# Latent heads: the rotated query's two halves stacked in one 128-row tile, and gate/value weights used in runs of sixteen products

## The chip, the cores and the metric

The kernel runs on one core of one Trainium2 chip. A core has five engines that each work through their own queue in order: TensorE (PE) multiplies matrices, with its weight loads shown as a row of their own (PEld); VectorE (DVE) and ScalarE (ACT) work element by element; GpSimd (POOL) does a little at the start; SyncE (SP) issues the transfers from the large memory. They wait for each other through semaphores only. The metric is the device time of one execution in microseconds; the kernel before has a median of 2402.7 us over three executions (2402.11 to 2403.8).

## What is computed

A decoder trunk of two layers over 256 tokens of width 2048, all in float32. Layer 0 is dilated window attention (three groups of eight heads) with a gated ConvFFN. Layer 1 is latent attention (twelve heads) over a shared key/value latent, and again a gated ConvFFN. Both also attend to 256 memory tokens. Cut to what the change touches:

```python
# layer 1: a query has a 128-wide part and a rotated 64-wide part; the rotated key is one for all heads
c      = rmsnorm(x, kv_g_norm) @ kv_w_dkv
c_kv   = rmsnorm(c[..., :512], kv_g_latent)
k_rope = rope(c[..., 512:], positions)                       # 64 wide, shared by the 12 heads
k_nope = (c_kv @ kv_w_uk).reshape(B, S, 12, 128)
q      = (cq @ b_w_uq[i]).reshape(B, S, 12, 128 + 64)
q_rope = rope(q[..., 128:], positions)
s = (einsum('bqhe,bkhe->bhqk', q_nope, k_nope)
     + einsum('bqhe,bke->bhqk', q_rope, k_rope)) * scale     # causal mask, softmax, times v

# both layers: the gated ConvFFN
g  = h @ w_gate
gc = conv_b + sum_j shift(g, j) * conv_w[j]
y  = (silu(gc) * (h @ w_val)) @ w_down
```

## The kernel before

**Numbers in two parts.** Every float32 operand is split into hi, its value rounded to the format that TensorE takes (fp32r), and lo, the rest. A product a·b is computed as hi·hi + hi·lo + lo·hi, three passes that add up in one PSUM bank; lo·lo is left out. Activations sit in tiles `op` of [128, 2, 256]: part, then token. Weights come from memory in chunks of 1 MB into a ring of three `raw` buffers and are split there into pieces of [128, 1024]: ACT writes `hi` (L445), DVE writes `lo` (L446), into a ring of four buffers each (`SPLIT_BUFS`). Piece i+4 can be split only when TensorE is done with piece i (`done_piece`).

**How the work is laid out.** `units()` lists the work; each unit is a weight matrix's column block with its pieces. What hangs on a unit (evacuating its bank, rotation, softmax) is recorded as small functions with a due time on a heap; `tick`, called after a product or a few, fires those that are due by the planner's own clock. So the order on each engine is fixed when the program is built, by planned times, and each engine then keeps to it whatever really takes longer.

**Gate and value.** For each of 44 column blocks per layer `unit_gv` takes four pieces: gate and value for the first eight k-tiles, gate and value for the last eight. A wide product multiplies a hi weight with both parts of an activation (512 columns, two of the three passes in one); a narrow one multiplies a lo weight with the hi part (256 columns). Both layers together have 88 such units, 176 halves. In two of them (`inter`, the first of each layer) the runs are of four, since their activations arrive while they run. `unit_wide`, which makes queries and keys of layer 0, has the same products in runs of sixteen wide and sixteen narrow.

**The latent heads.** For each group of four heads come the units `uk` (keys), `uv` (values), `uqr` (rotated queries, two heads side by side in the 128 rows of a bank: 64 rows each) and `uq` (the other part of the query). `rope` rotates a bank and `hilo` splits the result into an `op` tile ("qr", pair). The shared rotated key ("krT") has its 64 rows twice, in rows 0 to 63 and again in 64 to 127, since the unit `kr` loads the same weight columns twice. `mla_scores` then makes a head's scores by `causal_scores`: for the first 128 queries against 128 keys, and for the second against 256 keys, three products over 128 rows (qn·kn) and three over the head's 64 rows (qr·krT). The scores go through mask and maximum (DVE), exponential and scaling (ACT), transposes (PE, into `pth`), and the product with v (PE).

Of the kernel before, what the change touches and what calls it, by code (L numbers as in the profile page):

```python
# [11 lines left out]
F32 = mybir.dt.float32  # L12
F32R = mybir.dt.float32r
I32 = mybir.dt.int32
AF = mybir.ActivationFunctionType
ALU = mybir.AluOpType
AX = mybir.AxisListType

P = 128
T = 256  # L20
D = 2048
KD = D // P
DH = 128
# [4 lines left out]
NOPE = 128  # L28
# [21 lines left out]
LAT_S = 0.5  # L50
PBUFS = 12


# [141 lines left out]
class Core:  # L195
# [467 lines left out]
    def unit_gv(self, ui, u):  # L663
        a = [self.get("acc"), self.get("acc")]
        ops = u["ops"]
        for half in range(2):
            w = [self.take(ui)]
            if u["inter"]:
                w.append(self.take(ui))
                order = [(gv, range(k0, k0 + 4)) for k0 in (0, 4) for gv in range(2)]  # L670
            else:
                order = [(gv, range(8)) for gv in range(2)]
            for gv, ks in order:
                if gv == len(w):
                    self.done_piece()
                    w.append(self.take(ui))
                hi, lo = w[gv]
                for k in ks:
                    X = self.need(ops[8 * half + k])
                    self.mm(a[gv], hi[:, k * P:(k + 1) * P], X.rearrange("p a b -> p (a b)"), 512, half == 0 and k == 0, False)  # L680
                    self.tick()
                for k in ks:
                    X = self.need(ops[8 * half + k])
                    self.mm(a[gv][:, :T], lo[:, k * P:(k + 1) * P], X[:, 0, :], T, False, half == 1 and k == 7)
                    self.tick()
            self.done_piece(2 if u["inter"] else 1)
        _, l, f = u["name"]
        if f == NF - 1:
            self.put(*[("h", 10 + l, k) for k in range(KD)])
        if ("R", 10 + l) in self.T:  # L690
            self.gate(l, f, a)
        else:
            self.at(self.t, lambda: self.gate(l, f, a), keys=[("R", 10 + l)], urgent=True)
# [243 lines left out]

    def rope(self, o, key, half, cos, sin, then, scale=None, wide=False):
        sw, r = self.get("fs"), self.get("fs")
# [17 lines left out]
        def s2():  # L957
            t = self.op(key)
            e = self.hilo(t, T, r, psum=False)
            self.give("fs", r)  # L960
            if then:
                then(e)

        self.at(e + LAT_S, s1)

    def ev_q(self, name, h, o):
# [10 lines left out]
    def a_scores(self, half, g, h):  # L977
# [4 lines left out]
        pi = self.get("p")  # L982
        nm, e = self.causal_scores([(q, k, slice(0, P))], self.ptiles[pi], g, DH ** -0.5, ms)
        self.put(("q", half, g, h), ("k", half, g, h))
# [9 lines left out]
    def causal_scores(self, prods, p, mask, scale, ms):  # L994
        bank = self.get("wk")
        for tt in range(2):
            n = P * (tt + 1)
            o = bank[:, tt * P:tt * P + n]
            qs = slice(tt * P, (tt + 1) * P)
            steps = [(q[rows, i, qs], k[rows, j, 0:n]) for q, k, rows in prods for i, j in ((0, 0), (0, 1), (1, 0))]  # L1000
            for s, (a, b) in enumerate(steps):
# [256 lines left out]
    def ev_uqr(self, name, h, o):  # L1258
        self.rope(o, ("qr", 2 * name[1] + h), ROPE // 2, self.cosB, self.sinB, None)

# [6 lines left out]
    def mla_scores(self, h):  # L1267
        rows = slice((h % 2) * ROPE, (h % 2 + 1) * ROPE)
        pi = self.get("p")
        p = self.ptiles[pi]  # L1270
        ms, l, rl = self.st(2), self.st(2), self.st(2)
        nm, e = self.causal_scores([(self.T[("qn", h)], self.T[("kn", h)], slice(0, P)),
                                    (self.T[("qr", h // 2)], self.T[("krT",)], rows)], p, 3, (NOPE + ROPE) ** -0.5, ms)
        self.put(("qn", h), ("kn", h))
# [99 lines left out]
```

## Time and profile before

| | |
|---|---|
| median of three executions | 2402.7 us |
| the profiled execution: its own time, and its span | 2397.88 us, 2396.0 us |
| busy: PE, PEld, DVE, ACT | 99%, 86%, 66%, 55% of the span |
| mean granted TensorE clock | 0.996 of full speed |
| chain that ended last, by engine | PE 95%, ACT 2%, DVE 1%, DMA 1% |
| layer 0 attention; its FFN | about 55 to 515 us; 595 to about 1330 us |
| latent attention of layer 1 (units uk, uv, uqr, uq) | about 1450 to 1570 us |
| FFN of layer 1 | 1655 us to the end |

The timeline view has one row for a run of like instructions: start, length, engine, line, output and inputs by name, shape (rows x columns), count; in brackets the idle time before it and who ended it. A row's length includes the last instruction's way through the array, so the time of a run is read from its start to the next row's start. `acc<-op,hi` with 512 columns is a wide product, `acc<-op,lo` with 256 a narrow one, `wk<-op,op` are scores, `wk<-pth,op` is attention times v, `wk<-cst,pt` are transposes. The view by windows gives for a stretch each engine's busy time and the granted clock (PEclk).

### The profile page before, as it was taken

The page shows a single profiled execution, that of the slowest core. Times are in us where ns is not written, and L with a number is a line of the kernel's source. Part 1 is how long each engine was busy: PE and PEld are TensorE (multiplying, and loading weights), DVE is VectorE, ACT ScalarE, POOL GpSimd, SP SyncE. Part 2 cuts the span into 40 slices and gives each one's busy share as a digit, 9 for nine tenths or more (in the row PEclk, how much of TensorE's full clock was granted, in tenths as well). Part 3 has the DMA queues.
Part 4 walks back from the last instruction along what each step waited for, and adds up shares of the span by engine and source line. Part 5 has one row for each costly group of instructions (what it writes and reads, how often), then busy time and mean ns, then how long its engine had stood idle before and what let it go on. Part 6 is the DMA issues. An engine that isn't in the chain of part 4 may idle for free.

```text
span 2396.0 us, 33043 instructions
## 1 busy us (share of the span) xinstructions
PE 2377.3 (99%) x12896; PEld 2060.3 (86%) x12896; DVE 1585.0 (66%) x2439; ACT 1310.3 (55%) x2161; POOL 65.6 (3%) x78
## 2 busy tenths in 40 slices
PE   8999999999999999999999999999999999999998
PEld 8988888888888888888888888888888888888887
DVE  7677776665777567765776665656776567755765
ACT  6765665665655445543555656755554345544554
POOL 7300000000000000000000000000000000000000
PEclk9999999999999999999999999999999999999999
DMA  8454444544554555545555553235555555555553
GB/s 324 172 190 176 182 153 176 183 169 159 193 189 183 191 194 192 192 181 200 184 193 183 187 220 141 109 137 181 190 191 188 193 210 184 192 193 193 187 182 141
DMA packets 64749, 441.98 MB, mean 184 GB/s; under 512 B 7248, under 2 KB 7760, under 8 KB 12496
## 3 DMA queue, kind: packets, MB, share of 16 engines
q1 hardware_dynamic: 64592, 439.87, 50.4%
q8 instruction: 101, 1.65, 0.3%
q14 instruction: 56, 0.46, 0.0%
HBM read 437.75 MB, written 2.10 MB: 184 GB/s over the span
## 4 chain that ended last, share of the span: by engine, by line
PE 95%; ACT 2%; DVE 1%; DMA 1%; issue 0%; ACTq 0%; SPq 0%; DVEq 0%
PE acc L336 91%; PE wk L336 3%; DMA raw<-w 1%; PE wk L344 1%; DVE lo L361 1%; ACT hi L348 0%; ACT pt L348 0%; DVE op L361 0%; ACT fs L348 0%; ACT op L348 0%; DVE op L373 0%; DVE fs L361 0%; DVE pth L361 0%; ACT pth L348 0%; ACT junk L348 0%
## 5 line engine op out<-in xcount | busy, mean ns | idle before, releaser
L361 DVE TENSOR_TENSOR lo<-raw,hi 128x1024 fp32r<-128x1024 f32 (+1 forms) x816 | 1000.2, 1230 | 652.5 <-ACT hi L348 626.9
L348 ACT ACTIVATE hi<-raw 128x1024 fp32r<-128x1024 f32 (+1 forms) x816 | 857.5, 1057 | 764.3 <-PE acc L336 638.6
L336 PE MATMUL acc<-op,hi 128*128 128x512 f32 (+1 forms) x4112 | 998.7, 382 | 2.3 <-DVE op L361 2.3
L336 PEld LDWEIGHTS acc<-op,hi 128*128 128x128 f32 x4112 | 732.6, 189 | 125.0 <-DVE op L361 2.0
L336 PE MATMUL acc<-hi,op 128*128 128x512 f32 x2544 | 801.6, 392 | 0.8 <-DVE op L361 0.8
L336 PE MATMUL acc<-op,lo 128*128 128x256 f32 x3912 | 568.6, 282 | 0.8 <-DVE lo L361 0.8
L336 PEld LDWEIGHTS acc<-op,lo 128*128 128x128 f32 x3912 | 539.0, 191 | 33.5 <-DVE lo L361 1.0
L336 PEld LDWEIGHTS acc<-hi,op 128*128 128x128 f32 x2544 | 479.6, 189 | 100.2 <-DVE op L361 1.6
L336 PE MATMUL acc<-lo,op 128*128 128x512 f32 x1272 | 497.1, 391 | 0.9 <-DVE lo L361 0.9
L336 PEld LDWEIGHTS acc<-lo,op 128*128 128x128 f32 x1272 | 239.9, 189 | 49.0 <-DVE lo L361 1.7
L348 ACT ACTIVATE op<-fs 128x256 fp32r<-128x256 f32 x143 | 59.9, 419 | 119.5 <-DVE fs L361 118.9
L361 DVE TENSOR_TENSOR op<-fs,op 128x256 fp32r<-128x256 f32 x143 | 60.6, 424 | 64.3 <-ACT op L348 63.8
L348 ACT ACTIVATE fs<-scr 64x256 f32<-64x256 f32 x96 | 40.1, 418 | 91.5 <-DVE scr L361 90.6
L373 DVE SCALAR_TENSOR_TENSOR fs<-gpad,sml,fs 128x256 f32<-128x256 f32 x176 | 84.8, 482 | 3.1
L361 DVE TENSOR_TENSOR fs<-acc,fs 128x256 f32<-128x256 f32 x176 | 73.4, 417 | 0.0
L348 ACT ACTIVATE fs<-acc 128x256 f32<-128x256 f32 (+1 forms) x204 | 67.0, 373 | 0.4
L361 DVE TENSOR_TENSOR fs<-fs,fs 128x256 f32<-128x256 f32 x143 | 60.3, 421 | 1.9
L336 PE MATMUL wk<-op,op 128*128 128x128 f32 (+1 forms) x336 | 54.1, 295 | 0.0
L348 ACT ACTIVATE fs<-gpad,sml 128x256 f32<-128x256 f32 x88 | 51.9, 589 | 1.7 <-DVE gpad L361 1.6
L336 PEld LDWEIGHTS wk<-op,op 128*128 128x128 f32 x336 | 47.4, 195 | 6.1 <-issue 0.2
L348 ACT ACTIVATE pt<-pt,stat 128x128 f32<-128x128 f32 (+1 forms) x112 | 48.2, 455 | 0.9 <-DVE stat L366 0.9
L361 DVE TENSOR_TENSOR x<-acc,x 128x512 f32<-128x512 f32 (+1 forms) x66 | 41.2, 666 | 3.5 <-PE acc L336 3.5
(107 smaller groups left out, 879.0 us busy)
## 6 DMA issues: line engine op xcount, KB each, us to landing
raw<-w SPq DMA_DIRECT2D x407, 1024.0 KB, 4.8
raw<-w SPq DMA_DIRECT2D x8, 512.0 KB, 4.6
x<-x SPq DMA_DIRECT2D x4, 512.0 KB, 8.4
out<-x SPq DMA_DIRECT2D x8, 256.0 KB, 2.5
x<-w SPq DMA_DIRECT2D x5, 256.0 KB, 4.9
scr<-gfin SPq DMA_DIRECT2D x4, 256.0 KB, 6.5
cst<-cst SPq DMA_DIRECT2D x1, 640.0 KB, 6.7
raw<-w SPq DMA_DIRECT2D x2, 256.0 KB, 3.1
```

Source lines behind the costliest of these rows:

```text
L336: self.nc.tensor.matmul(out, lhsT, rhs, start=start, stop=stop, skip_group_check=True)
L344: self.nc.tensor.transpose(out, in_, self.ident)
L348: self.nc.scalar.activation(out, in_, func, **kw)
L361: self.nc.vector.tensor_tensor(out, a, b, op)
L373: self.nc.vector.scalar_tensor_tensor(out, a, s1, b, op0, op1)
```

## The change

Three things. `unit_gv` takes both pieces of a half at once and issues the eight wide gate products, the eight wide value products, then the eight narrow gate and the eight narrow value products; pieces are given back after the narrow run of each. For the rotated queries `rope` is called with `stack=True`: instead of one split of 128 rows into hi and lo, head b of the pair (rows 64b to 64b+63) gets its hi part in its own rows of plane b of the tile, and its lo part in the other 64 rows of the same plane; two ACT and two DVE instructions of 64 rows instead of one each of 128. And `causal_scores` takes a list of terms per operand pair: for qr·krT now two products over all 128 rows, plane b of the query tile against hi and against lo of the key, so that hi and lo of the query are multiplied in one pass (lo·lo comes with it). Everything else in the planner stays as it was, but its clock runs differently, and so some orders move.

```diff
+THREE = ((0, 0), (0, 1), (1, 0))
...
         for half in range(2):
-            w = [self.take(ui)]
+            w = [self.take(ui), self.take(ui)]
+            runs = [(gv, range(8)) for gv in range(2)]
             if u["inter"]:
-                w.append(self.take(ui))
-                order = [(gv, range(k0, k0 + 4)) for k0 in (0, 4) for gv in range(2)]
-            else:
-                order = [(gv, range(8)) for gv in range(2)]
-            for gv, ks in order:
-                if gv == len(w):
-                    self.done_piece()
-                    w.append(self.take(ui))
-                hi, lo = w[gv]
+                runs = [(gv, range(k0, k0 + 4)) for k0 in (0, 4) for gv in range(2)]
+            for gv, ks in runs:
                 for k in ks:
                     X = self.need(ops[8 * half + k])
-                    self.mm(a[gv], hi[:, k * P:(k + 1) * P], X.rearrange("p a b -> p (a b)"), 512, half == 0 and k == 0, False)
+                    self.mm(a[gv], w[gv][0][:, k * P:(k + 1) * P], X.rearrange("p a b -> p (a b)"), 512, half == 0 and k == 0, False)
                     self.tick()
-                for k in ks:
+            for gv in range(2):
+                for k in range(8):
                     X = self.need(ops[8 * half + k])
-                    self.mm(a[gv][:, :T], lo[:, k * P:(k + 1) * P], X[:, 0, :], T, False, half == 1 and k == 7)
+                    self.mm(a[gv][:, :T], w[gv][1][:, k * P:(k + 1) * P], X[:, 0, :], T, False, half == 1 and k == 7)
                     self.tick()
-            self.done_piece(2 if u["inter"] else 1)
+                self.done_piece()
...
-            e = self.hilo(t, T, r, psum=False)
+            e = self.stack(t, r) if stack else self.hilo(t, T, r, psum=False)
...
+    def stack(self, t, r):
+
+        rows = [slice(i * ROPE, (i + 1) * ROPE) for i in range(2)]
+        for b in range(2):
+            e = self.act(t[rows[b], b, :], r[rows[b]], AF.Copy, T)
+        for b in range(2):
+            e = self.tt(t[rows[b ^ 1], b, :], r[rows[b]], t[rows[b], b, :].bitcast(F32), ALU.subtract, T, e)
+        self.rdy[id(t)] = e + LAT_S
+        return e
...
-            steps = [(q[rows, i, qs], k[rows, j, 0:n]) for q, k, rows in prods for i, j in ((0, 0), (0, 1), (1, 0))]
+            steps = [(q[:, i, qs], k[:, j, 0:n]) for q, k, terms in prods for i, j in terms]
...
-        self.rope(o, ("qr", 2 * name[1] + h), ROPE // 2, self.cosB, self.sinB, None)
+        self.rope(o, ("qr", 2 * name[1] + h), ROPE // 2, self.cosB, self.sinB, None, stack=True)
...
-        nm, e = self.causal_scores([(self.T[("qn", h)], self.T[("kn", h)], slice(0, P)),
-                                    (self.T[("qr", h // 2)], self.T[("krT",)], rows)], p, 3, (NOPE + ROPE) ** -0.5, ms)
+        nm, e = self.causal_scores([(self.T[("qn", h)], self.T[("kn", h)], THREE),
+                                    (self.T[("qr", h // 2)], self.T[("krT",)], ((h % 2, 0), (h % 2, 1)))], p, 3, (NOPE + ROPE) ** -0.5, ms)
```

What this does to the order of instructions is shown at three places. First, TensorE in the middle of a gate/value half, before and after (`hi` and `lo` with a number are buffers of the split rings, `acc_141` gathers the gate and `acc_142` the value):

```order
6374 L336 MATMUL acc_141<-op_76,hi_67 128x512
6375 L336 MATMUL acc_141<-op_91,hi_67 128x512
6376 L336 MATMUL acc_141<-op_92,hi_67 128x512
6377 L336 MATMUL acc_141<-op_86,lo_71 128x256
6378 L336 MATMUL acc_141<-op_83,lo_71 128x256
6379 L336 MATMUL acc_141<-op_117,lo_71 128x256
```

```order
6374 L337 MATMUL acc_141<-op_76,hi_67 128x512
6375 L337 MATMUL acc_141<-op_91,hi_67 128x512
6376 L337 MATMUL acc_141<-op_92,hi_67 128x512
6377 L337 MATMUL acc_142<-op_86,hi_68 128x512
6378 L337 MATMUL acc_142<-op_83,hi_68 128x512
6379 L337 MATMUL acc_142<-op_117,hi_68 128x512
```

After the eighth wide gate product stood the first narrow gate product; now the first wide value product stands there, from the next buffer, and the narrow gate products follow it eight places later.

Second, TensorE where the first group of latent heads is scored, before and after (`op_109` is the shared rotated key, `op_116` and `op_87` are two pairs of rotated queries, the other `op` tiles the 128-wide parts of keys and queries; the columns are keys):

```order
7606 L336 MATMUL wk_147<-op_80,op_98 128x128 x3
7607 L336 MATMUL wk_147<-op_109,op_116 128x128 x3
7608 L336 MATMUL wk_147<-op_80,op_98 128x256 x3
7609 L336 MATMUL wk_147<-op_109,op_116 128x256 x3
7610 L336 MATMUL wk_148<-op_86,op_110 128x128 x3
7611 L336 MATMUL wk_148<-op_109,op_116 128x128 x3
7612 L336 MATMUL wk_148<-op_86,op_110 128x256 x3
7613 L336 MATMUL wk_148<-op_109,op_116 128x256 x3
7614 L336 MATMUL wk_145<-op_83,op_85 128x128 x3
7615 L336 MATMUL wk_145<-op_109,op_87 128x128 x3
7616 L336 MATMUL wk_145<-op_83,op_85 128x256 x3
7617 L336 MATMUL wk_145<-op_109,op_87 128x256 x3
```

```order
7606 L337 MATMUL wk_147<-op_80,op_98 128x128 x3
7607 L337 MATMUL wk_147<-op_109,op_116 128x128 x2
7608 L337 MATMUL wk_147<-op_80,op_98 128x256 x3
7609 L337 MATMUL wk_147<-op_109,op_116 128x256 x2
7610 L337 MATMUL wk_148<-op_86,op_110 128x128 x3
7611 L337 MATMUL wk_148<-op_109,op_116 128x128 x2
7612 L337 MATMUL wk_148<-op_86,op_110 128x256 x3
7613 L337 MATMUL wk_148<-op_109,op_116 128x256 x2
7614 L337 MATMUL wk_145<-pth_134,op_82 128x256 x3
7615 L337 MATMUL wk_145<-pth_134,op_113 128x256 x3
7616 L337 MATMUL wk_146<-op_81,op_75 128x128 x3
7617 L337 MATMUL wk_146<-op_109,op_87 128x128 x2
```

A head has ten products instead of twelve. Three heads stood in a row, now two, and a product of the memory attention (`pth_134`) stands between them and the third.

Third, ACT at about the same time, before and after (`op_87<-fs_159` is the split of a rotated pair, `pth_133<-wk` evacuates the transposes of a memory head, `pt_124` to `pt_131` with `stat` as an output are exponentials, `hi` is a weight piece):

```order
1262 L348 ACTIVATE op_87<-fs_159 128x256
1263 L348 ACTIVATE pt_126<-pt_126,stat 128x256
1264 L348 ACTIVATE pt_132<-pt_132,stat 128x256
1265 L348 ACTIVATE op_77<-acc_144 128x256
1266 L348 ACTIVATE hi_69<-raw_63 128x1024
1267 L348 ACTIVATE op_100<-acc_141 128x256
1268 L348 ACTIVATE op_114<-wk_146 128x256
1269 L348 ACTIVATE pth_133<-wk_148 128x512
1270 L348 ACTIVATE pt_125<-pt_125,stat 128x256
1271 L348 ACTIVATE pt_131<-pt_131,stat 128x256
1272 L348 ACTIVATE pt_124,stat<-pt_124,stat 128x128
1273 L348 ACTIVATE pt_124,stat<-pt_124,stat 128x256
```

```order
1262 L349 ACTIVATE op_87<-fs_159 64x256 x2
1263 L349 ACTIVATE pt_126<-pt_126,stat 128x256
1264 L349 ACTIVATE pt_132<-pt_132,stat 128x256
1265 L349 ACTIVATE op_77<-acc_144 128x256
1266 L349 ACTIVATE hi_69<-raw_63 128x1024
1267 L349 ACTIVATE op_100<-acc_141 128x256
1268 L349 ACTIVATE op_114<-wk_145 128x256
1269 L349 ACTIVATE pt_125<-pt_125,stat 128x256
1270 L349 ACTIVATE pt_131<-pt_131,stat 128x256
1271 L349 ACTIVATE hi_66<-raw_63 128x1024
1272 L349 ACTIVATE pth_133<-wk_147 128x512
1273 L349 ACTIVATE pt_124,stat<-pt_124,stat 128x128
```

The split of the rotated pair has become two instructions; the scalings of the memory head (`pt_125`, `pt_131`) and a weight piece (`hi_66`) now stand ahead of the transposes' evacuation, not behind it. Over the whole program ACT and DVE each have six instructions more.

More of the change, by code (lines that the diff above doesn't have):

```diff
@@ L935, in xcol, with rope @@
             self.at(e + LAT_S + 0.01 * bp, lambda bp=bp: go(bp), urgent=True, wk=1, op=2 * len(sets))
-    def rope(self, o, key, half, cos, sin, then, scale=None, wide=False):
+    def rope(self, o, key, half, cos, sin, then, scale=None, wide=False, stack=False):
         sw, r = self.get("fs"), self.get("fs")
@@ L982, in a_scores @@
         pi = self.get("p")
-        nm, e = self.causal_scores([(q, k, slice(0, P))], self.ptiles[pi], g, DH ** -0.5, ms)
+        nm, e = self.causal_scores([(q, k, THREE)], self.ptiles[pi], g, DH ** -0.5, ms)
         self.put(("q", half, g, h), ("k", half, g, h))
@@ L1267, in mla_scores @@
     def mla_scores(self, h):
-        rows = slice((h % 2) * ROPE, (h % 2 + 1) * ROPE)
         pi = self.get("p")
```

## The prediction

> **What bounds the kernel now.** I read the page first: busy times, then the chain that ended last.
>
> ```profile
> PE 2377.3 (99%) x12896; PEld 2060.3 (86%) x12896; DVE 1585.0 (66%) x2439; ACT 1310.3 (55%) x2161; POOL 65.6 (3%) x78
> PE 95%; ACT 2%; DVE 1%; DMA 1%; issue 0%; ACTq 0%; SPq 0%; DVEq 0%
> ```
>
> TensorE is busy for 99% of the span and carries 95% of the chain; ACT and DVE are idle a third of the time or more. So time is won where TensorE takes less, stage by stage, as long as another engine doesn't become the last to finish there. The change touches TensorE in two stages: gate/value and the latent heads. For both I read the timeline of TensorE; a run's time goes from its start to the next row's start, since a row's length holds the pipeline's tail.
>
> **Scores of the latent heads.** The first row, from the chain in order of time, is a score group of layer 0: six products over 128 rows. The others, from the timeline, are all twelve latent heads in their runs (12 products a head, half of them over 64 rows), and what stands behind them.
>
> ```profile
> 151.25 0.69 PE wk L336 x6
> ...
> 1482.29 6.48 PE L336 MATMUL wk<-op,op 128*128 128x128 f32 x36
> 1488.69 1.65 PE L336 MATMUL wk<-pth,op 128*128 128x256 f32 x6
> 1490.14 3.44 PE L336 MATMUL wk<-op,op 128*128 128x128 f32 x12
> 1493.51 1.11 PE L344 MATMUL wk<-cst,pt 128*128 128x128 f32 x4
> ...
> 1498.42 0.40 PE L336 MATMUL acc<-lo,op 128*128 128x512 f32 x1
> ...
> 1498.89 0.87 PE L336 MATMUL wk<-pth,op 128*128 128x256 f32 x6
> 1499.59 0.60 PE L344 MATMUL wk<-cst,pt 128*128 128x128 f32 x4
> 1499.95 0.48 PE L336 MATMUL acc<-hi,op 128*128 128x512 f32 x1
> ...
> 1521.14 2.08 PE L336 MATMUL wk<-op,op 128*128 128x128 f32 x12
> 1523.15 0.55 PE L344 MATMUL wk<-cst,pt 128*128 128x128 f32 x3
> 1523.45 2.11 PE L336 MATMUL wk<-op,op 128*128 128x128 f32 x12
> 1525.49 0.50 PE L336 MATMUL acc<-hi,op 128*128 128x512 f32 x1
> ...
> 1526.98 4.08 PE L336 MATMUL wk<-op,op 128*128 128x128 f32 x24
> 1531.00 1.60 PE L336 MATMUL wk<-pth,op 128*128 128x256 f32 x12
> 1532.44 0.44 PE L336 MATMUL acc<-hi,op 128*128 128x512 f32 x1
> ...
> 1554.99 8.43 PE L336 MATMUL wk<-op,op 128*128 128x128 f32 x48
> 1563.35 2.82 PE L336 MATMUL wk<-pth,op 128*128 128x256 f32 x12
> ...
> 1570.09 0.40 PE L336 MATMUL acc<-lo,op 128*128 128x512 f32 x1
> ```
>
> The runs take 6.40, 3.37, 2.01, 2.04, 4.02 and 8.36 us, 26.2 us for twelve heads; an undisturbed head takes 2.01. Were its products like those of layer 0 (0.69 / 6 = 0.115 us each) it would take 1.38. The other 0.63 must come from the products over 64 rows or from going to and from them, since that alone sets them apart: a gate/value unit changes its operands with every product and pays nothing like it.
>
> The change makes ten products a head, all over 128 rows, five with 128 columns and five with 256. The layer 0 group is three and three, so the mix is the same: 10 x 0.115 = 1.15 us, 13.8 for twelve heads. **Saved: 26.2 - 13.8 = 12.4 us.** Bounds: if only the count mattered, 24 x 0.115 = 2.8 us; the other end is the 12.4 itself, since nothing in the rows makes a 128-row product cheaper.
>
> The Trainium skill ("TensorE: Matmul & The Clock Gate", section "Why this matters for your kernels") speaks against this: "K=32 single mm = same time as K=128". By that rule only the 2.8 us would come. The trace differs: 0.168 us a product where half have 64 rows (2.01 / 12), 0.115 where none has.
>
> **The granted clock.** The view by windows shows that the clock is halved behind the two longest score runs:
>
> ```profile
> 1485.00:1490.00 5.00, 5.00 (x27) 4.16 (x27) 1.79 (x11) 0.00 (x0) 0.00 (x0) 0.79 0.33 128
> 1490.00:1495.00 5.00, 5.00 (x20) 4.22 (x20) 1.24 (x6) 0.68 (x2) 0.00 (x0) 0.50 0.00 0
> 1565.00:1570.00 5.00, 5.00 (x16) 4.19 (x16) 0.85 (x2) 4.11 (x18) 0.00 (x0) 0.52 0.01 2
> ```
>
> The columns are PE, PEld, DVE, ACT and POOL busy, then PEclk. It falls inside the runs of 6.40 and 8.36 us and stays whole behind that of 4.02, with PE shown busy throughout (5.00 of 5.00). So a long stretch of these slow products seems to count as little work. After the change the longest row of heads is three (the order has runs of 2, 1, 1, 2, 2, 3 and 1), 3.45 us by the price above, and denser. I take it that the clock stays whole. Outside the scores this is worth: from 1488.69, six products by v in 1.45 us where 0.70 is the whole-clock time (1498.89 to 1499.59); from 1493.51 to 1498.42 four transposes and ten wide products in 4.91, where 0.36 + 10 x 0.228 = 2.64 is normal (0.228 is a sixteenth of a 3.65 us run below); together 3.0. From 1563.35 to 1570.09, 6.74 us for twelve products by v (1.44 at 1531.00) and ten wide ones (2.28): again 3.0. **Saved: 6.0 us**, or nothing if the clock falls all the same.
>
> The Trainium skill ("TensorE: Matmul & The Clock Gate", section "HAM oscillation — how this bites in real kernels") names idle gaps of over about 3.4 us as what brings the clock down. The trace shows no such gap here, the drops come in a busy row; by the rule they would have another cause and could stay, which is the third rival.
>
> **Gate and value.** Layer 0's wide units already have runs of sixteen; two rows of the one, two of the other kind:
>
> ```profile
> 231.14 3.82 PE L336 MATMUL acc<-op,hi 128*128 128x512 f32 x16
> 234.79 2.08 PE L336 MATMUL acc<-op,lo 128*128 128x256 f32 x16
> ...
> 253.41 3.82 PE L336 MATMUL acc<-op,hi 128*128 128x512 f32 x16
> ...
> 864.94 2.00 PE L336 MATMUL acc<-op,hi 128*128 128x512 f32 x8
> ...
> 901.25 2.00 PE L336 MATMUL acc<-op,hi 128*128 128x512 f32 x8
> ```
>
> Between 231.14 and 253.41 lie four rounds of 16 + 16 products: 5.567 us each. Between 864.94 and 901.25 lie thirteen rounds of 8 + 8: 2.793, so 5.586 for what will be one round. **Saved: 0.019 us a half, 176 halves, 3.3 us.** The two `inter` units go from runs of four to 16 wide and 16 narrow too, a few hundredths each; not counted.
>
> What could eat it is weight pieces that come late, as both are now held longer. The timeline of a half, all engines:
>
> ```profile
> 999.02 2.00 PE L336 MATMUL acc<-op,hi 128*128 128x512 f32 x8
> ...
> 1001.06 1.06 ACT L348 ACTIVATE hi<-raw 128x1024 fp32r<-128x1024 f32 x1 [1.19 <-PE acc L336]
> ...
> 1002.15 1.23 DVE L361 TENSOR_TENSOR lo<-raw,hi 128x1024 fp32r<-128x1024 f32 x1 [0.60 <-ACT hi L348]
> ...
> 1010.19 1.09 PE L336 MATMUL acc<-op,hi 128*128 128x512 f32 x4
> ```
>
> The piece used from 999.02 is replaced by 1003.38 and used again four rounds later, at 1010.19: 6.8 us to spare. The gate's lo is now freed after wide, wide, narrow and not after wide, narrow, so one wide run of 1.84 us later; the value's hi is wanted 0.95 us sooner. About 5 us are left, and ACT waits for TensorE there, not the reverse. Cost: nothing; uncovered, it would be the excess over those 5 us in each half. ACT's reordering of a gate step before a `hi` (under 1 us) lies in the same slack. The chunk is freed by its second lo, as before, so DMA issues move by little.
>
> **The stack.** Per pair one ACT and one DVE instruction become two of each, over 64 rows:
>
> ```profile
> L348 ACT ACTIVATE fs<-scr 64x256 f32<-64x256 f32 x96 | 40.1, 418 | 91.5 <-DVE scr L361 90.6
> L361 DVE TENSOR_TENSOR op<-fs,op 128x256 fp32r<-128x256 f32 x143 | 60.6, 424 | 64.3 <-ACT op L348 63.8
> ```
>
> On ACT 64 rows cost what 128 do (0.418 us). For DVE there is no 64-row row; the bounds are half of 0.424 and all of it, and by ACT's example I take all. Six pairs: 2.5 us more on each engine, 0.84 a group of four heads. It matters only where ACT is what TensorE waits for, and that is here:
>
> ```profile
> 1494.71 0.60 ACT L348 ACTIVATE pth<-wk 128x512 fp32r<-128x512 f32 x1 [3.94 <-PE wk L344]
> ...
> 1513.53 0.51 PE L336 MATMUL acc<-op,hi 128*128 128x256 f32 x2 [0.51 <-DVE op L361]
> ...
> 1500.00:1520.00 20.00, 19.49 (x153) 18.77 (x152) 16.43 (x35) 18.59 (x45) 0.00 (x0) 1.00 0.29 100
> ```
>
> ACT waits for transposes until 1494.71, then works almost without a pause until TensorE runs into it at 1513.53 (start to start 0.67 late). Queued behind that evacuation on ACT are exponentials, rotations and weight pieces of the next units. Counted from the first score at 1482.29, TensorE will be 5.2 us sooner by four heads (9.77 - 4.6) and 3.0 by the clock: at the spot by 1504.7 (1512.86 - 8.2). ACT's run starts 12.4 us after the first score; with three heads (3.45), six products by v (0.70), six wide ones (1.37) and four transposes (0.36) ahead of it in the new order, it starts after about 6.0, 6.4 sooner, and ends by 1513.5 - 6.4 + 0.84 = 1508.0. TensorE waits 3.3 instead of 0.67: **2.6 given back**; the next group, whose ACT stretch is not shortened, gives back 0.8. **Lost: 3.4 us**, between nothing (today's waits stay) and rival one.
>
> **Sum.** 12.4 + 6.0 + 3.3 - 3.4 = 18.3 us. The durations are those of the profiled execution, 2397.88 us with a span of 2396.0, which would become 2379.6; the median shown is 4.8 us above it, and the difference applied there gives **2384.4 us**.
>
> **The rivals.**
> 1. ACT and DVE pace the whole latent stage: the clock's 6.0 us is lost as waiting, since ACT is as busy behind both drops (1500 to 1520: 18.59 of 20; 1565 to 1570: 4.11 of 5), and two groups of stack (1.7) come on top. Gain 12.4 + 3.3 - 1.7 = 14.0, 2388.7. Against it: in 1485 to 1495 ACT works 0.68 of 10 us, so it has room to start earlier.
> 2. The order closes today's waits as well: nothing lost, 21.7 gained, 2381.0, and down to 2379 if waits like that at 1513.53 go.
> 3. The clock falls again, behind three heads in a row or elsewhere: gain 12.3, 2390.4. Against it: 4.02 us of the sparser products didn't bring it down.
> 4. The change doesn't do what it says, since the 0.63 us a head comes from changing the operand pair and not from 64 rows, and long runs need not stop the drop: 2.8 + 3.3, 2396.6. Against it: products by v change both operands midway (1.44 for twelve, no step of that size).
> 5. Slower: gate/value halves wait for weights. Both pieces must lie split when a half begins, and DVE's two lo stand back to back. It decides from 15.0 / 176 = 0.085 us a half beyond the gain there; at 0.15, 26 us are lost and 15 gained, 2414. Against it: the 5 us to spare.
>
> **How the numbers follow.** Forecast 0.58; rivals 0.16, 0.08, 0.08, 0.06 and 0.04. The range 2378 to 2392 holds the forecast and the first three. A measurement of this kernel tells about 0.2% (5 us) from no change. Faster is the forecast and the first three, 0.90, with half of the fourth, which lies near the border: 0.93; same 0.04 (the other half, and a mild fifth); slower 0.03.
>
> **What would show it.** Scores: no row with 64 rows, runs of 10, 20 and 30 products at 1.15 us a head. Clock: 1.00 in all windows from 1450 to 1600. Gate/value: rounds of 5.567. Waits: TensorE waiting for DVE `op` between the groups, about 3 us more than now. I am wrong if a head still takes over 1.5 us, if the halved clock is there again, or if TensorE shows waits on `lo` in the FFN.

## The result, and the profile after

The changed kernel takes 2380.58 us (median of four executions, 2379.49 to 2380.85); the kernel before, run beside it, 2402.62 us (2402.11 to 2403.8). The ratio is 0.9907, with a 95% interval of 0.9892 to 0.9922. The profiled execution took 2380.38 us with a span of 2378.4 us, against 2397.88 and 2396.0 before.

The page of the kernel after, busy times and the chain that ended last:

```profile
PE 2357.3 (99%) x12872; PEld 2050.2 (86%) x12872; DVE 1573.8 (66%) x2445; ACT 1310.8 (55%) x2167; POOL 67.6 (3%) x78
PE 96%; ACT 1%; DVE 1%; DMA 1%; issue 0%; ACTq 0%; SPq 0%; DVEq 0%
```

TensorE bounds the kernel as before. Its busy time fell by 20.0 us and the span by 17.6. Cut at the same instructions of both traces (the first wide product of a gate/value block, the first of the down-projection, the first latent score, the last product), the two profiled executions differ so:

| stage | before, us | after, us | difference |
|---|---|---|---|
| start of the program to the first FFN | 595.20 | 597.27 | +2.07 |
| gate/value of layer 0 | 666.84 | 665.26 | -1.58 |
| from there to the first latent score | 220.25 | 220.90 | +0.65 |
| first latent score to the second FFN | 172.69 | 155.49 | -17.20 |
| gate/value of layer 1 | 666.83 | 665.27 | -1.56 |
| from there to the last product | 65.08 | 65.08 | 0 |

The first row is no effect of the change: over all kernels of this study that start lay between 595.2 and 598.1 us, and a second profile of the kernel before had 597.75.

**The latent stage.** TensorE's timeline of the kernel after, the first heads and the longest row of heads:

```profile
1483.43 2.47 PE L337 MATMUL wk<-op,op 128*128 128x128 f32 x20
1485.74 0.88 PE L337 MATMUL wk<-pth,op 128*128 128x256 f32 x6
1486.45 1.31 PE L337 MATMUL wk<-op,op 128*128 128x128 f32 x10
1487.60 0.40 PE L337 MATMUL acc<-hi,op 128*128 128x512 f32 x1
...
1545.05 3.67 PE L337 MATMUL wk<-op,op 128*128 128x128 f32 x30
1548.56 0.81 PE L337 MATMUL wk<-pth,op 128*128 128x256 f32 x6
```

From start to start, 20 products take 2.31 us, 10 take 1.15 and 30 take 3.51: 1.15 to 1.17 us a head, 14.05 for twelve, where it was 26.20. The clock, by windows of 20 us, first of the kernel before:

```profile
1480.00:1500.00 20.00, 19.55 (x90) 15.97 (x88) 8.25 (x30) 7.31 (x24) 0.00 (x0) 0.74 0.33 125
1500.00:1520.00 20.00, 19.49 (x153) 18.77 (x152) 16.43 (x35) 18.59 (x45) 0.00 (x0) 1.00 0.29 100
1560.00:1580.00 20.00, 20.00 (x88) 16.59 (x88) 7.42 (x21) 11.40 (x32) 0.00 (x0) 0.83 0.15 54
```

and of the kernel after:

```profile
1480.00:1500.00 20.00, 19.14 (x136) 17.34 (x135) 14.81 (x46) 15.06 (x44) 0.00 (x0) 1.00 0.33 129
1500.00:1520.00 20.00, 19.09 (x158) 18.64 (x157) 17.13 (x42) 16.38 (x42) 0.00 (x0) 1.00 0.47 159
1520.00:1540.00 20.00, 18.12 (x128) 16.48 (x128) 14.09 (x37) 16.68 (x44) 0.00 (x0) 1.00 0.30 106
1560.00:1580.00 20.00, 20.00 (x106) 17.07 (x105) 10.82 (x14) 9.94 (x17) 0.00 (x0) 1.00 0.45 156
```

The drops (0.74 and 0.83) are gone; the clock is whole in all windows from 1440 to 1600. In the first 20 us TensorE now issues 136 products instead of 90, and ACT works 15.06 us instead of 7.31.

**Gate and value.** Two rows of TensorE's timeline after, six rounds of 16 wide and 16 narrow products apart:

```profile
869.33 3.82 PE L337 MATMUL acc<-op,hi 128*128 128x512 f32 x16
...
902.73 2.46 PE L337 MATMUL acc<-op,hi 128*128 128x512 f32 x10
```

(902.73 - 869.33) / 6 = 5.567 us a round, where it was 5.586.

**The waits.** The places in the latent stage where TensorE stands idle, in the timeline of the kernel after (the bracket is the idle time shown and who ended it):

```profile
1481.16 0.50 PE L337 MATMUL acc<-hi,op 128*128 128x512 f32 x1 [0.36 <-DVE op L362]
...
1482.62 0.51 PE L337 MATMUL acc<-hi,op 128*128 128x512 f32 x1 [0.51 <-DVE op L362]
...
1504.32 0.50 PE L337 MATMUL acc<-op,hi 128*128 128x256 f32 x2 [0.91 <-DVE fs L362]
...
1528.43 0.47 PE L337 MATMUL acc<-op,hi 128*128 128x256 f32 x2 [0.34 <-ACT pt L349]
...
1537.48 0.50 PE L337 MATMUL acc<-hi,op 128*128 128x512 f32 x1 [1.54 <-DVE op L362]
```

Counted from start to start, less a product's normal 0.12 or 0.23 us, they are 0.52, 0.68, 1.07, 0.50 and 1.70 us. Before there were 0.61 ahead of the first score and 0.67, 1.02 and 0.47 behind it; beside the one at 1513.53, which the prediction shows, these are

```profile
1481.47 0.50 PE L336 MATMUL acc<-hi,op 128*128 128x512 f32 x1 [0.45 <-DVE op L361]
...
1539.15 0.50 PE L336 MATMUL acc<-op,hi 128*128 128x256 f32 x2 [0.86 <-DVE op L361]
...
1547.82 0.50 PE L336 MATMUL acc<-hi,op 128*128 128x512 f32 x1 [0.31 <-DVE op L361]
```

So the waits behind the first score grew from 2.16 to 3.27 us, and one more, of 0.68, came ahead of it: 1.8 us in all.

### The profile page after: what moved, and what is told of

Read it like the earlier page. It is cut to its first block, busy times and chain, and to the rows that moved or that the text cites. A ratio compares the mean times of both kernels' runs of the same rounds, so it can differ in the third digit from the quotient of the medians.

```text
span 2378.4 us, 33089 instructions
## 1 busy us (share of the span) xinstructions
PE 2357.3 (99%) x12872; PEld 2050.2 (86%) x12872; DVE 1573.8 (66%) x2445; ACT 1310.8 (55%) x2167; POOL 67.6 (3%) x78
## 4 chain that ended last, share of the span: by engine, by line
PE 96%; ACT 1%; DVE 1%; DMA 1%; issue 0%; ACTq 0%; SPq 0%; DVEq 0%
PE acc L337 92%; PE wk L337 3%; PE wk L345 1%; DMA raw<-w 1%; DVE lo L362 0%; ACT pt L349 0%; ACT fs L349 0%; ACT hi L349 0%; DVE op L374 0%; DVE op L362 0%; ACT op L349 0%; ACT pth L349 0%; DVE fs L362 0%; DVE pth L362 0%; ACT junk L349 0%
## 5 line engine op out<-in xcount | busy, mean ns | idle before, releaser
L349 ACT ACTIVATE hi<-raw 128x1024 fp32r<-128x1024 f32 (+1 forms) x816 | 836.1, 1050 | 448.5 <-PE acc L337 423.9
L337 PE MATMUL acc<-op,hi 128*128 128x512 f32 (+1 forms) x4112 | 964.0, 381 | 2.2 <-DVE op L362 0.9
L337 PEld LDWEIGHTS acc<-op,hi 128*128 128x128 f32 x4112 | 744.2, 189 | 135.0 <-DVE fs L362 1.1
L337 PE MATMUL acc<-op,lo 128*128 128x256 f32 x3912 | 540.5, 283 | 0.0
L337 PEld LDWEIGHTS acc<-op,lo 128*128 128x128 f32 x3912 | 514.9, 191 | 18.3
L349 ACT ACTIVATE fs<-fs 128x256 f32<-128x256 f32 x88 | 36.7, 418 | 157.9 <-DVE fs L374 157.9
L349 ACT ACTIVATE op<-fs 128x256 fp32r<-128x256 f32 (+1 forms) x149 | 62.0, 416 | 97.2 <-DVE fs L362 96.5
L362 DVE TENSOR_TENSOR op<-fs,op 128x256 fp32r<-128x256 f32 (+1 forms) x149 | 63.1, 424 | 64.4 <-ACT op L349 63.5
L349 ACT ACTIVATE fs<-acc 128x256 f32<-128x256 f32 (+1 forms) x204 | 76.1, 375 | 22.0 <-PE acc L337 21.6
L337 PE MATMUL wk<-op,op 128*128 128x256 f32 (+1 forms) x312 | 42.6, 279 | 0.0
```

What stands on the lines that cost most here:

```text
L337: self.nc.tensor.matmul(out, lhsT, rhs, start=start, stop=stop, skip_group_check=True)
L349: self.nc.scalar.activation(out, in_, func, **kw)
L362: self.nc.vector.tensor_tensor(out, a, b, op)
```

## The experiments

All were made from the kernel before or the kernel after, and timed beside the kernel before on the same chip. Its medians there were 2401.2, 2401.54 and 2399.96 us in three sets. "Stage" below is the time from the first latent score to the second FFN.

### The kernel before, once more

No edit. The profiled execution shown of before was 4.8 us under its median; this run asks what sets it apart.

> The kernel before, unchanged. In its profiled execution the time was 2397.88 us, in its timed ones 2402.1 to 2403.8; the changed kernel shows no such difference (2380.4 and 2380.6). Theory A (halvings of the clock differ from one execution to the next, since how a window of the clock's monitor lies over the long score runs is chance): executions near 2402.5 show a lower mean granted clock than 0.996, about 0.994 (one more drop of about 10 us), those near 2398 show 0.996. Theory B (something else, such as the start): all show 0.996 and their spans still differ by 4 to 5 us.

Measured: 2401.45 us (2398.22 to 2403.49, ten executions), ratio 1.0, interval 0.9991 to 1.0009. The profiled execution took 2400.24 us, 2.4 more than the one shown, with the same two drops (10.24 and 6.83 us long); the first FFN began 2.55 us later, which is all of the difference. So this pair differs by the start (theory B). Over all executions the time goes with the clock (theory A), which each timed execution reports as well. The 42 executions of the kernel before that ran beside the kernels of this study:

| mean granted clock | executions | us |
|---|---|---|
| 0.999 | 2 | 2392.9, 2393.8 |
| 0.997 | 6 | 2396.3 to 2398.1 |
| 0.996 | 3 | 2397.9 to 2399.7 |
| 0.995 | 17 | 2399.3 to 2404.0 |
| 0.994 | 12 | 2401.2 to 2405.5 |
| 0.992, 0.993 | 2 | 2406.9, 2404.7 |

The kernel before costs about 8.6 us more at its usual 0.994 to 0.995 (mean of 29 executions) than at 0.999 (mean of two). By its clock of 0.996, the profiled execution shown had shorter drops than most. The four executions of the kernel after are at 0.998 and 0.999.

### The stack alone

The kernel before with `stack`, the two products over 128 rows and nothing else; gate/value as it was.

```diff
+            e = self.stack(t, r) if stack else self.hilo(t, T, r, psum=False)
...
+            steps = [(q[:, i, qs], k[:, j, 0:n]) for q, k, terms in prods for i, j in terms]
...
+                                    (self.T[("qr", h // 2)], self.T[("krT",)], ((h % 2, 0), (h % 2, 1)))], p, 3, (NOPE + ROPE) ** -0.5, ms)
```

> Only the stacked rotated queries and their two products over 128 rows; gate/value as before, in runs of eight. My theory: scores and clock are worth 12.4 + 6.0 - 3.4 = 15.0 us by the prediction, 17 by the changed kernel's trace, so 2384 to 2386 against 2402.6, clock 1.00 in the latent stage. Rival (only the count of products matters): 2.8 us, 2399.8.

Measured: 2383.07 us (2381.56 to 2383.69), ratio 0.9923, interval 0.9908 to 0.9938. The stage takes 155.51 us, the scores 14.05, and gate/value takes 666.83 and 666.81, as before. The clock doesn't fall in the windows where it fell before:

```profile
1480.00:1500.00 20.00, 19.13 (x138) 17.52 (x137) 15.49 (x47) 15.11 (x42) 0.00 (x0) 1.00 0.35 132
1560.00:1580.00 20.00, 20.00 (x108) 17.07 (x107) 10.46 (x16) 11.16 (x20) 0.00 (x0) 1.00 0.44 158
```

The waits are those of the kernel after to 0.01 us. So all of the gain in the latent stage comes from the stack, and none of it needs the other order in gate/value.

### Gate and value alone

The kernel before with the new order of `unit_gv`, the latent heads as they were.

```diff
-            w = [self.take(ui)]
+            w = [self.take(ui), self.take(ui)]
+            runs = [(gv, range(8)) for gv in range(2)]
```

> Only gate/value in runs of sixteen; scores as before with six products over 64 rows a head. My theory: 176 halves at 0.019 us, so 3.3 us: 2399.3; rounds of 16 + 16 products of 5.567 us in the trace; the latent stage as before with its halved clock. Rival (late weight pieces): TensorE waits on lo in the FFN and the time is 2402.6 or more.

Measured: 2398.08 us (2394.80 to 2402.31, ten executions), ratio 0.9985, interval 0.9975 to 0.9994. TensorE's timeline has five rounds between these rows, and the halved clock is there, in the window below:

```profile
869.68 3.82 PE L336 MATMUL acc<-op,hi 128*128 128x512 f32 x16
...
897.51 3.82 PE L336 MATMUL acc<-op,hi 128*128 128x512 f32 x16
```

```profile
1490.00:1495.00 5.00, 5.00 (x20) 4.32 (x20) 1.24 (x6) 0.38 (x1) 0.00 (x0) 0.50 0.00 0
```

27.83 / 5 = 5.566 us a round; the gate/value parts of the two FFNs take 665.29 and 665.27, 3.1 us less than before. Nothing shows a weight piece coming late. Against the medians beside them, the stack alone gains 18.1 us and this part alone 3.1, together 21.2 of the 22.0 of the whole change. The drops are both 10.24 us long, the stage 174.68 and the scores 28.91: the drops reach further into the score runs than in the profile shown, by the place at which they fall.

### Three products over 128 rows

The kernel after with a third product per rotated pair, over 128 rows (the second one twice), so that a head has twelve products as before, but none over 64 rows.

```diff
-                                    (self.T[("qr", h // 2)], self.T[("krT",)], ((h % 2, 0), (h % 2, 1)))], p, 3, (NOPE + ROPE) ** -0.5, ms)
+                                    (self.T[("qr", h // 2)], self.T[("krT",)], ((h % 2, 0), (h % 2, 1), (h % 2, 1)))], p, 3, (NOPE + ROPE) ** -0.5, ms)
```

> The changed kernel with three products over 128 rows for the rotated part, not two: the product with the key's lo part is made twice, so the scores have that small term twice. Twelve products a head as before the change, none over 64 rows. My theory (64 rows, or going to and from them, cost 0.63 us a head): a head takes 12 x 0.115 = 1.38 us. Rival 1 (only the count matters): 2.01 us as before. Rival 2 (changing the operand pair costs it): about 2.0 us.

Measured in one execution: 2384.1 us. TensorE's timeline, a row of three heads and one of four:

```profile
1520.38 4.38 PE L337 MATMUL wk<-op,op 128*128 128x128 f32 x36
1524.61 1.49 PE L337 MATMUL wk<-pth,op 128*128 128x256 f32 x12
...
1548.43 5.79 PE L337 MATMUL wk<-op,op 128*128 128x128 f32 x48
1554.06 1.50 PE L337 MATMUL wk<-pth,op 128*128 128x256 f32 x12
```

4.23 us for 36 products is 1.41 a head and 5.63 for 48 is 1.41: twelve products over 128 rows take what the price of layer 0 gave (1.38), and not 2.01. No clock drop in the latent stage. Of the 12.15 us that the scores lost, 2.78 come from having ten products instead of twelve (16.83 - 14.05) and 9.4 from having none over 64 rows. Of these 9.4, about 2.1 are the halved clock inside the score runs of before (26.2 less twelve undisturbed heads of 2.01); 7.3 are the products over 64 rows at the whole clock.

### Two products over 64 rows

The kernel before, whose rotated pair has the first two of its three products over 64 rows.

```diff
-            steps = [(q[rows, i, qs], k[rows, j, 0:n]) for q, k, rows in prods for i, j in ((0, 0), (0, 1), (1, 0))]
+            steps = [(q[rows, i, qs], k[rows, j, 0:n]) for q, k, rows in prods for i, j in (((0, 0), (0, 1), (1, 0)) if rows.stop - rows.start == P else ((0, 0), (0, 1)))]
```

> The kernel before, but the rotated part of the scores with two products over 64 rows, not three (the product of the query's lo part with the key's hi part is left out). Ten products a head as in the changed kernel, four of them over 64 rows. My theory (going to and from 64 rows costs about 0.15 us each time, four times a head, whatever the number of products between): 2.01 - 2 x 0.115 = 1.78 us a head. Rival (each 64-row product is dear by itself, 0.63 / 6 = 0.105 us more): 1.15 + 4 x 0.105 = 1.57 us. Rival 2 (only the count matters): 1.15 us, as in the changed kernel.

Measured in one execution: 2398.36 us. A head in TensorE's timeline:

```profile
1522.20 1.84 PE L336 MATMUL wk<-op,op 128*128 128x128 f32 x10
1523.97 0.55 PE L344 MATMUL wk<-cst,pt 128*128 128x128 f32 x3
```

1.77 us for ten products, where ten over 128 rows take 1.15. A head goes four times between 128 and 64 rows, with three products a visit as with two: (2.01 - 1.38) / 4 = 0.157 us before, (1.77 - 1.15) / 4 = 0.155 here. The extra time hangs on the changes and not on the number of the products over 64 rows. The single products in the trace of the kernel before show the same, outside the drops and from start to start. From the second product over 64 rows to the third it takes 0.111 us with 128 columns and 0.118 with 256, as it does over 128 rows (0.112 and 0.120). The step to the other row count takes 0.20 to 0.21 us, and the step behind that 0.16 (128 columns) or 0.22 (256 columns). The drops are there again (10.24 us each, the stage 171.25).

### Heads apart

The kernel before with a head's scores planned no closer than 3.0 us to the last head's, by the planner's clock; the work is the same.

```diff
+        if self.t < getattr(self, "next_scores", 0.0):
+            self.at(self.next_scores, lambda: self.mla_scores(h), wk=1, p=1)
+            return
+        self.next_scores = self.t + 3.0
```

> The kernel before with its products over 64 rows, but two heads are scored no closer than 3 us by the planner's clock, so other products stand between. My theory (a long stretch of these sparse products brings the clock down): no halved clock in the latent stage, a head still 2.0 us, time 5 to 7 us less than the kernel before (2395 to 2397). Rival (each 64-row product counts as no work, or the drop has another cause): the clock falls as before and the time is about 2401.

Measured: 2390.74 us (2390.37 to 2392.57), ratio 0.9959, interval 0.9946 to 0.9972; better than expected. The window in which the clock stood at 0.50 before, in this kernel:

```profile
1490.00:1495.00 5.00, 5.00 (x32) 4.22 (x31) 2.88 (x9) 2.53 (x10) 0.00 (x0) 1.00 0.00 0
```

No drop, with products over 64 rows as before and 1.95 to 2.01 us a head. The stage takes 163.98 us, 8.7 less than before. 2.66 of that are in the scores (parts of the drops lay in the score runs, and 0.06 a head came off), 1.07 are waits: those behind the first score went from 2.16 to 1.09 us (0.29, 0.48 and 0.32). The last two of them:

```profile
1541.81 0.51 PE L336 MATMUL acc<-op,hi 128*128 128x256 f32 x2 [0.32 <-DVE fs L361]
...
1545.36 0.50 PE L336 MATMUL acc<-hi,op 128*128 128x512 f32 x1 [0.15 <-DVE op L361]
```

The rest is 5.0 us. Counted product by product in both traces, the drops of before cost 6.0 us outside the scores, as predicted, and 1.0 us comes back here in many small delays, each under 0.25 us, mostly between weight products.

### Long and dense

The kernel after, every product of the latent scores issued twice (the scores are doubled), so that three heads in a row without a 64-row product take as long as a run behind which the clock fell.

```diff
...
+            if len(steps) == 5:
+                for s, (a, b) in enumerate(steps):
+                    self.nc.tensor.matmul(o, a, b, start=False, stop=s == 4, skip_group_check=True)
```

> The changed kernel with every score product of the latent heads made twice (the scores are doubled), so that up to 60 products over 128 rows, about 6.9 us, stand in a row, as long as the runs behind which the clock fell before (6.40 and 8.36 us). My theory (it is the sparse 64-row products that count as little work): the clock stays whole through the latent stage. Rival (any long run of small products brings it down): halved for 7 to 10 us behind the run of 60. Time: twelve more heads' worth, about 14 us above the changed kernel, so 2394, or 2399 with drops.

Measured in one execution: 2394.25 us. The longest row, 60 products between these two rows of the timeline, and the clock:

```profile
1554.32 0.72 PE L337 MATMUL wk<-op,op 128*128 128x128 f32 x5
...
1561.30 0.81 PE L337 MATMUL wk<-pth,op 128*128 128x256 f32 x6
```

```profile
1555.00:1560.00 5.00, 5.00 (x46) 5.00 (x46) 3.12 (x12) 0.21 (x1) 0.00 (x0) 1.00 0.58 188
1560.00:1565.00 5.00, 5.00 (x42) 4.87 (x42) 1.77 (x10) 2.86 (x13) 0.00 (x0) 1.00 0.05 21
```

6.98 us of score products in a row, longer than the 6.40 behind which the clock fell before, and it stays whole. So length alone did not bring it down; with the run before, neither did the products over 64 rows alone. In these runs it took both. This run was executed once, though, and 2 of the 42 executions of the kernel before kept 0.999 as well. Whether it is the half-empty rows or the slower sequence of products that counts is not separated.

The run shows a second thing. Its order is that of the kernel after, and the four heads of the first group take 4.6 us more; the wait behind them is 1.06 us where it was 1.07. The wait does not depend on how long the scores are: ACT and DVE get their work from the scores, and so are early or late together with TensorE.

### Alternating wide and narrow

The kernel after, gate/value with one wide and one narrow product in turn: the shortest runs instead of the longest.

```diff
-            runs = [(gv, range(8)) for gv in range(2)]
+            runs = [(gv, range(k0, k0 + 1)) for gv in range(2) for k0 in range(0, 8, 1)]
...
```

> The changed kernel, but gate/value alternates one wide and one narrow product. In runs the first five wide products after a narrow one take 25 ns more together than later ones, the first narrow one 8 ns less. Theory A (the dear places are the second to fifth wide product of a run, so a run of one has only the first, +6 and -7 ns): a round of 16 + 16 takes about 5.54 us, 0.03 less than in runs of sixteen, 5 us less in all: about 2376. Theory B (each change from narrow to wide costs its 17 to 20 ns however short the run): sixteen changes a half, not one, 15 x 0.018 x 176 = 47 us more: about 2428.

Measured: 2394.90 us (2393.14 to 2398.67, ten executions), ratio 0.9979, interval 0.9966 to 0.9992. Two rows of the timeline, 96 wide and 96 narrow products apart:

```profile
866.85 0.39 PE L337 MATMUL acc<-op,hi 128*128 128x512 f32 x1
...
900.76 0.40 PE L337 MATMUL acc<-op,hi 128*128 128x512 f32 x1
```

33.91 / 6 = 5.65 us for 16 and 16; the two gate/value parts take 672.85 and 672.89. So 16 + 16 products cost 5.65, 5.586 and 5.567 us in runs of one, eight and sixteen. With 32, 4 and 2 changes of kind that is 2.4 ns a change between one and eight (66 ns for 28) and 9.5 between eight and sixteen (19 for 2). A change has no fixed price; fewer of them are better each time. Neither of the two expectations gave this number.

### Heads apart, on top of the change

The kernel after with the lines of "heads apart", at 3.0 us and at 2.0 us.

> After's kernel, with the latent heads' scores never planned closer together than 3.0 us by the planner's own clock. Nothing is left out. Theory (the order of before crowded the heads, and what ACT and DVE had to do for them came in bursts that TensorE then waited for; heads_apart showed this for the old scores): of after's waits in the latent stage behind the first score, 3.27 us, about 0.5 stay, so 2.5 to 2.8 us are gained on after: about 2377.9. Rival (with scores of 1.15 us a head the bursts are bound by the rotations of the units, not by the heads, and apart they only begin their softmax later): the waits stay at 3 us or grow, 2380.5 to 2382.

> The same with 2.0 us instead of 3.0. Theory: between after and the kernel with 3.0 us, waits of 0.5 to 2 us in the latent stage behind the first score, 2378 to 2379.5. Rival: as after, 2380.5 or more.

Measured: 2378.53 us at 3.0 (2378.18 to 2380.38, five executions), ratio 0.9912, interval 0.9894 to 0.9931; 2380.85 us at 2.0 (2379.99 to 2382.2), ratio 0.9921, interval 0.9905 to 0.9937. With 3.0 the stage takes 154.18 us, 1.3 less than after. The waits behind the first score are 1.87 us, not the 0.5 expected: 0.61, 0.43 and 0.83. The first of them in the timeline:

```profile
1503.77 0.51 PE L337 MATMUL acc<-op,hi 128*128 128x256 f32 x2 [0.45 <-DVE fs L362]
```

With 2.0 they are 3.75 and nothing is gained, as the rival had it. The intervals of the kernel after and of the one at 3.0 overlap; what is shown is 1.3 us less in the stage of one trace, not a faster kernel.

## Why the prediction was right, and which terms were off

Forecast 2384.4 us, measured 2380.58, within the range; the mechanism was the forecast one. Step by step:

**Scores: 12.4 us predicted, 12.15 measured.** The price of layer 0 held (1.15 us a head). About 2.1 us of it are halved clock inside the score runs, which the prediction counted with the scores; at the whole clock the scores gain about 10. Rival 4, that the 0.63 us a head comes from changing the operands, fell with the three products over 128 rows: as many changes of operands, 1.41 us. The Trainium skill ("TensorE: Matmul & The Clock Gate", section "Why this matters for your kernels") says that a single product over 32 rows takes as long as one over 128. For the products themselves the trace agrees, with 64 rows in place of 32: 0.111 us against 0.112 with 128 columns. What the rule leaves out here is the change between the two, about 0.16 us each time; by the rule only the 2.78 us would have come.

**The clock: 6.0 us predicted, 6.2 in the two profiles** (17.20 - 12.15 + 1.11, what the scores and waits behind the first score leave of the stage; counted inside the drops, 6.0). It stayed whole in the latent stage, and rival 3 fell. The Trainium skill ("TensorE: Matmul & The Clock Gate", section "HAM oscillation — how this bites in real kernels") has idle gaps of over about 3.4 us bring the clock down. In the kernel before, and again with gate/value alone, it fell with TensorE shown busy for 5.00 of 5.00 us; what removed it was spacing the sparse runs or making them dense.

**Gate/value: 3.3 us predicted, 3.14 measured**, from rounds of 5.567 us as said. Cost of later weight pieces: nothing predicted, and the FFN stages leave no room for one; rival 5 fell.

**The stack: as predicted.** The view of groups of the kernel after:

```profile
L362 DVE TENSOR_TENSOR op<-fs,op 64x256 fp32r<-64x256 f32 x12 | 5.0, 420 | 0.4
L349 ACT ACTIVATE op<-fs 64x256 fp32r<-64x256 f32 x12 | 5.0, 415 | 0.1
```

Over 64 rows DVE takes what it takes over 128 (420 ns against 424), the upper of the two bounds.

**Waits given back: 3.4 us predicted, 1.8 measured. This is the term that was mis-sized.** It was put together from 2.6 in the first group and 0.8 in the next; measured are 0.40 (1.07 against 0.67) in the first group, 0.71 (0.50 + 1.70 against 1.02 + 0.47) behind the next, and 0.65 ahead of the first score. So the 2.6 was far too large, the 0.8 about right, and the 0.65 was missing.

- The first group's wait is 1.07 us and not 3.3. The step took ACT's work behind the evacuation of the transposes as fixed and let TensorE run into its end. The evacuation began 6.7 us after the first score (1490.15), near the 6.0 predicted, but the row on ACT in the order shown with the change already had two scalings and a weight piece ahead of it, which the step did not take off; ACT then works 15.06 us in the first 20, not 7.31. What TensorE meets is a rotation at another place. The chain that ended at that wait:

```profile
1499.80 1.50 ACT pt L349 x4
1501.30 0.95 ACT hi L349
...
1503.43 0.38 ACT fs L349
...
1503.84 0.43 DVE fs L362
...
1504.32 1.69 PE acc L337 x12
```

  The scalings of exponentials and a weight piece stand ahead of the four copies that the rotation needs.
- The next group's largest wait is 1.70 us (1537.48), where DVE's split of a weight piece stands ahead of the `op` that TensorE needs:

```profile
1535.87 1.23 DVE L362 TENSOR_TENSOR lo<-raw,hi 128x1024 fp32r<-128x1024 f32 x1 [0.20 <-ACT hi L349]
...
1537.01 0.75 DVE L362 TENSOR_TENSOR op<-acc,op 128x256 fp32r<-128x256 f32 x2
```

- The 0.65 ahead of the first score was not in the sum. It is there in all seven kernels with the stack (220.86 to 220.90 us between FFN and first score) and in none without (220.18 to 220.25). DVE's timeline of the kernel after shows the two halves ahead of the `op` that TensorE waits for at 1481.16:

```profile
1479.78 0.87 DVE L362 TENSOR_TENSOR op<-fs,op 64x256 fp32r<-64x256 f32 x2
...
1480.68 0.42 DVE L362 TENSOR_TENSOR op<-acc,op 128x256 fp32r<-128x256 f32 x1
```

**Rivals 1 and 2** were the two ends for this term: 7.7 us given back, or nothing. By the first the stage would lose 10.7 us (12.4 - 1.7), by the second 18.4. It lost 17.2, nearer the second: TensorE and ACT became early together, as the doubled scores show. The measured 2380.58 us is even closer to rival 2's 2381.0 than to the forecast, but that is luck and not its mechanism: 1.8 us were given back, and the step from the profile to the median, next, hides them.

**From the profile to the median.** The sum was made against one execution and its difference applied to the median. By its clock that execution had shorter drops than most (0.996 against the usual 0.994 and 0.995), so a kernel without drops gains more against the median than against it. The measured medians lie 22.0 us apart, the profiled stages behind the start 19.7. The other 2.3 us are put down to the clock, since the starts cancel when the kernel before begins its first FFN as late as in its second profile (597.75); no profile of a usual execution shows it. In the execution shown the halved clock cost 8.1 us in all, 6.0 outside the scores and 2.1 in them. Without it the terms are 12.15 - 2.1 + 3.14 - 1.76 = 11.4 us, which would leave 10.6 of the 22.0 for the clock of a usual execution; the table above gives 8.6. Against the two executions of the kernel before that kept 0.999 (2393.4 on average) the kernel after gains 12.8 and not 11.4; this difference isn't placed. This step, some 2.3 us too small, and the waits, 1.6 too large, make up most of the 3.8 us by which the forecast was too high.

## What to carry to other kernels

Stacking two 64-row operands into one 128-row tile is worth more than the product it saves, because every change between 64 and 128 rows costs as much as a product or more; count the changes, not the products. A halved clock can stand in a window where TensorE is shown fully busy; here it went away by denser products or by spreading the sparse ones, with the same work. When TensorE becomes faster, ask whether the engine it will wait for gets its own input from the work that was shortened: then both are early, and little is given back.

## What the runs showed of the hardware that was not expected

- Going between products over 128 rows and over 64 costs about 0.16 us each time, whether two or three products follow (0.157 and 0.155 us); within a row over 128 rows a product of this mix takes 0.115 to 0.117. A product over 64 rows behind another of its kind takes what one over 128 rows takes (0.111 and 0.112 with 128 columns).
- In the profiled executions the clock was halved behind runs of 6.40 and 8.36 us of such mixed products, not behind 4.02 us of them, and not behind 6.98 us of products over 128 rows only. The drops were 6.83 or 10.24 us long, two or three times 3.41 us. Both profiles of the kernel before had one of each; with gate/value alone and with two products over 64 rows both were 10.24. That they differ between executions of one kernel is inferred from the timed executions, whose clock goes from 0.992 to 0.999 and whose time goes with it.
- A pause of two to three microseconds at the start of the program, where a weight piece comes late, was followed by a halved clock in three profiles and not in three others. The kernel after has

```profile
39.38 0.50 PE L337 MATMUL acc<-lo,op 128*128 128x512 f32 x1 [2.08 <-DVE lo L362]
```

  and the clock is halved from 40.54 us for 3.41. From one start to the next this pause takes 2.46 us; it is 2.79 and 2.49 with three products over 128 rows and with alternating products, with the same drop, but 2.53, 2.40 and 2.49 in the kernel before once more, with the stack alone and in the kernel after with heads 3.0 us apart, without one.
- What it costs to go between wide and narrow products grows with the length of the runs: 2.4 ns for each change saved from runs of one to eight, 9.5 from eight to sixteen.
